# First expert pair of a routed SwiGLU layer: three column blocks side by side, with the gather between them

## The chip, the cores and the metric

The kernel runs on one core of one Trainium2 chip. The metric is device time in microseconds (us) of one execution, as the median over runs. A profiled execution also gives a span, from the first to the last instruction of the program.

## The reference

One post-norm encoder layer in float32 over 512 tokens of width 1024: LayerNorm, a mixer (short gated convolution and windowed attention), a residual and a second LayerNorm, then the part that the change touches, a mixture of 16 experts in which each expert picks its own 64 tokens:

```python
def expert_choice_moe(x, w_router, w_gate, w_up, w_down):
    B, S, _ = x.shape
    cap = CAPACITY_FACTOR * S // N_EXPERTS
    logits = jnp.einsum('bsd,de->bse', x, w_router).astype(jnp.float32)
    aff = jax.nn.softmax(logits, axis=-1)
    top_val, top_idx = lax.top_k(jnp.swapaxes(aff, 1, 2), cap)
    xe = x[b_idx, top_idx]
    h = jax.nn.silu(jnp.einsum('becd,edf->becf', xe, w_gate)) * jnp.einsum('becd,edf->becf', xe, w_up)
    ye = jnp.einsum('becf,efd->becd', h, w_down) * top_val[..., None].astype(x.dtype)
    return jnp.zeros_like(x).at[b_idx, top_idx].add(ye)
```

A residual and a last LayerNorm follow. The expert weights are 16 x 3 x 1024 x 2048 floats, 402.7 MB.

## The kernel before, in words

**Stages.** The mixer runs first and streams its weights through SBUF pools that are closed behind it. Then come routing (ranks, thresholds and places of the tokens, on VectorE) and the experts, in eight pairs `p`. Two experts of a pair sit side by side in 64 + 64 columns.

**A pair.** `gather(p)` builds a one-hot matrix `oh1` in the tile `px_p` (VectorE, L895) and returns a list of steps: eight row blocks of gathered tokens (`g`, TensorE L903, each then copied into `xe`) and a transposed one-hot (`oht`, L918). The hidden width of 2048 goes in four blocks of columns `cb`. In a block there are eight weight units of 1 MB (gate and up alternate, `i`; four quarters of the depth, `kq`), and each is used by 8 TensorE matmuls (`pg`, `pu`, L993; the order lists count two column halves as one row of 4). After a block come `silu` on ScalarE (L1003), the product on VectorE (L1004), and a step `turn` that transposes `h` (`ht`, L1016). Then 16 units of the down projection (`d`, L1042), and the scatter (`sc`, L1055). So a pair has 48 units.

**What sets the order on TensorE.** All its instructions are pinned to the order in which the program is written. Side steps wait in the list `pend`; the loop over units pops some between two units. In pair 0, block 0 pops two after each up unit, so that gathers come in twos; all later blocks pop one after each gate unit. When the block `cb == 1` of pair 0 ends, `pend` gets four steps of `spread` (`ln`, L929: TensorE writes the gain and bias of the second LayerNorm into PSUM, ScalarE copies each to the tile `ln1`, L930; the first two steps are the gain, the last two the bias) and then `affine` (L971 to L974), eight GpSimd instructions that multiply the four token tiles `xt` by the gain and add the bias, in place. Pair 0 has gathered its rows before that and applies gain and bias to them by itself; all later pairs gather from the finished `xt`.

**Between the pairs.** At the end of the four blocks `gather(1)` is called, and two of its steps (`g_1_0`, `g_1_2`) and the last `turn` run at once, ahead of the first `d`. Its tile `px_1` lies in the buffer W0, where `ln1` lies until `affine` is done, so VectorE's L895 for pair 1 waits for the last of GpSimd's instructions.

**Loads.** SyncE issues the weight loads in the order of the list, and each waits for its place. Units 0 to 71 (`SMALL`) are loads of 1 MB into places of 8 KB a partition: E, R0 to R19, W2, W0, so 23 units fit at first. After that W0 and W2 hold other tiles, and R0 and R1 become the accumulator, so that a unit from the 45th on goes into the place of the one 19 earlier. From unit 72 on four buffers G0 to G3 of 4 MB each take a group of four units with one load; they lie on R2 to R17, four places each. So the load of units 72 to 75 (into G2) waits until unit 56 has been used, the next until unit 60, and the load of units 80 to 83 (into G0) until unit 67.

Of the kernel before, what the change touches and what calls it, by code (L numbers as in the profile page):

```python
# [22 lines left out]
KT = D // P  # L23
# [8 lines left out]
NCB = FF // 512  # L32
# [7 lines left out]
def encoder_layer(ctx: ExitStack, tc: tile.TileContext, x, ln0r, ln0c, w_in, conv_w, sink, w_ao, w_co, w_out,  # L40
                  ln1c, w_router, w_moe, ln2c, out):
    nc = tc.nc
# [3 lines left out]
    extra = ctx.enter_context(tc.tile_pool(name="extra", bufs=1))  # L46
# [5 lines left out]
    pin = tc.keep_in_program_order  # L52

    def shaped(t, shape):
        names = "abcd"[:len(shape)]
        return t[:, :int(np.prod(shape))].rearrange(f"p ({' '.join(names)}) -> p {' '.join(names)}",
                                                    **dict(zip(names, shape)))

    def wkt(i, shape, name):
        return shaped(wk.tile([P, 2048], F32, tag=f"W{i % 3}", name=name), shape)  # L60
# [7 lines left out]
    def pst(name):  # L68
        return psp.tile([P, 512], F32, tag="ps", name=name)

    def mmt(name):
        return mmp.tile([P, 512], F32, tag="mm", name=name)
# [264 lines left out]
    src, nm, _ = loads[0]  # L337
# [244 lines left out]

    UNITS, SMALL = 48, 72
    units, groups = {}, {}

    def load_unit(n, pool, tag):
        t = pool.tile([P, 2048], F32, tag=tag, name=f"w_{n}")
        p, m = n // UNITS, n % UNITS  # L590
        pin(nc.sync.dma_start(t, w_moe[p, m // 4][:, m % 4]))
        return t

    def fetch(p, m):

        n = UNITS * p + m
        if n < SMALL:
            if n not in units:
                units[n] = load_unit(n, *places.pop(0))
            return units.pop(n)  # L600
        if not big:
            small.close()
            big.extend(ctx.enter_context(tc.tile_pool(name=f"big{i}", bufs=1, reuse_waits="tile")) for i in range(4))
            rest = ctx.enter_context(tc.tile_pool(name="late", bufs=1, reuse_waits="tile"))
            for name, shape, dt in (("c6", [P, KT, NT, 32], F32R), ("n6", [P, NT, 32], F32R), ("rows6", [P, D], F32R),
                                    ("left6", [P, P], F32R), ("diag", [P, P], F32)):
                late[name] = rest.tile(shape, dt, name=name)
        g, j = m // 4, m % 4
        if j == 0:
            i = (n // 4) % 4  # L610
            t = big[i].tile([P, 4, 2048], F32, tag=f"G{i}", name=f"w_{p}_{g}")
            src = w_moe[p, g]
            if p < NPAIR - 1 or g < 4:
                pin(nc.sync.dma_start(t, src))
            for i in range(4 if p == NPAIR - 1 and g >= 4 else 0):
                if (g, i) != (UNITS // 4 - 1, 3):
                    pin(nc.sync.dma_start(t[:, i], src[:, i]))
                else:
                    ends, begin = shaped(t[:, i], [2, 4, 256]), shaped(src[:, i], [2, 4, 256])
                    for f, n in ((0, 2), (2, 1), (3, 1)):  # L620
                        pin(nc.sync.dma_start(ends[:, :, f:f + n, :], begin[:, :, f:f + n, :]))
            groups[p, g] = t
        return groups[p, g][:, j]
# [255 lines left out]
    slots = [(accp, "R0"), (accp, "R1")]  # L879
    for i in range(2, 20):  # L880
        slots.append((small.enter_context(tc.tile_pool(name=f"r{i}", bufs=1, reuse_waits="tile")), f"R{i}"))
    places = slots[:7] + [(wk, "W2")] + slots[7:8] + [(wk, "W0")] + slots[8:]
    places += [(extra, "E")] + slots + [(extra, "E")] + slots[2:] + [(extra, "E")] + slots[2:10]
    big = []
    for n in range(1, 23):
        units[n] = load_unit(n, *places.pop(0))

    def gather(p):
# [74 lines left out]
    pend = []  # L963
# [16 lines left out]
    for p in range(NPAIR):  # L980
        last = p == NPAIR - 1
        xe, ohT, takes = nxt
        pend[:0] = takes
        for cb in range(NCB):
            pss = [mmt(f"p{nm}_{p}_{cb}") for nm in "gu"]
            for kq in range(4):
                for i in range(2):
                    wt = shaped(fetch(p, 8 * cb + 2 * kq + i), [2, 2, 512])
                    for k in range(2):
                        kk = 2 * kq + k  # L990
                        for a in range(2):
                            hs = slice(64 * a, 64 * a + 64)
                            pin(nc.tensor.matmul(pss[i][hs, :], xe[:, kk, hs], wt[:, a, k, :], start=(kk == 0), stop=(kk == KT - 1)))  # L993
                    for _ in range(2 * i if p == cb == 0 else 1 - i):
                        if pend:
                            pend.pop(0)()
            if last and cb == 1:
                ln2 = wkt(2, [1, D], "ln2")
                pend.extend(spread(ln2, 4, 2))
                ln2 = ln2[:, 0, :]  # L1000
                pend.extend(last_rows())
            hb = tmpt([512], f"h_{p}_{cb}")
            nc.scalar.activation(hb, pss[0], AF.Silu)  # L1003
            nc.vector.tensor_tensor(hb, hb, pss[1], OP.mult)  # L1004
            if p == 0 and cb == 1:
                ln1 = wkt(0, [2, D], "ln1")
                pend.extend(spread(ln1, 2))
                pend.append(affine)

            def turn(cb=cb, hb=hb, p=p):  # L1010
                if cb == 0:
                    hTs[p] = wkt(2 + 2 * p, [FF // P, P], f"hT_{p}")
                hT = hTs[p]
                ps = pst(f"ht_{p}_{cb}")
                for i in range(4):
                    pin(nc.tensor.transpose(ps[:, i * P:(i + 1) * P], hb[:, i * P:(i + 1) * P], ident))  # L1016
                nc.scalar.copy(hT[:, 4 * cb:4 * cb + 4, :].rearrange("p k c -> p (k c)"), ps)

            pend.append(turn)
            if last and cb == 2:  # L1020
                def begin(i):
                    def go():
                        ps = pst(f"end{i}")
                        pin(nc.tensor.matmul(ps, ident, acc[i][:, :, 768:1024], start=True, stop=False))
                        ends.extend(ps[:, 256 * t:256 * t + 256] for t in range(2))
                    return go
                pend.extend(begin(i) for i in range(2))
        if not last:
            nxt = gather(p + 1)
            for _ in range(2):  # L1030
                nxt[2].pop(0)()
            flush()
        nq, width = (4, 256) if last else (2, 512)
        for cq in range(nq):
            pd = mmt(f"d_{p}_{cq}")
            for fq in range(16 // nq):
                wt = shaped(fetch(p, 32 + 16 // nq * cq + fq), [2, nq, width])
                for ft in range(nq):
                    f = nq * fq + ft
                    for a in range(2):  # L1040
                        hs = slice(64 * a, 64 * a + 64)
                        pin(nc.tensor.matmul(pd[hs, :width], hTs[p][:, f, hs], wt[:, a, ft, :], start=(f == 0), stop=(f == 15)))  # L1042
                for _ in range(2):
                    if pend:
                        pend.pop(0)()
            ye = tmpt([width], f"ye_{p}_{cq}")
            nc.scalar.copy(ye, pd[:, :width])  # L1047
            if p == 0 and cq == 0:
                acc = [shaped(accp.tile([P, 2048], F32, tag=f"R{i}", name=f"acc{i}"), [2, D]) for i in range(2)]

            def scatter(t, p=p, cq=cq, ye=ye, ohT=ohT, width=width):
                def go():
                    cs = slice(cq * width, (cq + 1) * width)
                    ps = pst(f"sc_{p}_{cq}_{t}")
                    pin(nc.tensor.matmul(ps[:, :width], ohT[:, t * P:(t + 1) * P], ye, start=True, stop=True))  # L1055
                    a = acc[t // 2][:, t % 2, cs]
                    if p == 0:
                        nc.vector.scalar_tensor_tensor(a, xt[t][:, cs], ALPHA, ps[:, :width], op0=OP.mult, op1=OP.add)
                    else:
                        nc.vector.tensor_tensor(a, a, ps[:, :width], OP.add)  # L1060
                    if p == NPAIR - 1:
                        nc.vector.bn_stats(st2[:, t, cq, :], a)
                        nc.vector.tensor_tensor(a, a, ln2[:, cs], OP.mult)
                return go

            if last and cq == 0:
                pin(nc.scalar.preload_act_table(AF.Sqrt))
            if not (last and cq == 3):
                pend.extend(scatter(t) for t in range(NT))
# [96 lines left out]
```

## Time and profile before

| | us |
|---|---|
| median of 3 runs | 1443.61 (1443.17 to 1448.71) |
| the profiled execution, its own time | 1443.45 |
| its span | 1441.7 |
| TensorE busy in the span | 1365.8 (95%) |
| VectorE, ScalarE, GpSimd busy | 387.0, 290.5, 56.4 |

The profile has a page (busy time, 40 slices, the chain that ended last, the costliest groups) and a trace that answers by stretch, by engine and by tile. In a row of a stretch, "DMA share" is the mean busy share of the core's 16 DMA engines, and GB/s what they moved.

### The profile page before, as it was taken

What the parts mean: (1) busy time and instruction counts of PE and PEld (TensorE: products, weight loads), DVE (VectorE), ACT (ScalarE), POOL (GpSimd) and SP (SyncE); (2) the same over time, 40 slices, a digit from 0 to 9 for tenths busy, and PEclk for the clock granted to TensorE, in tenths of its full rate; (3) what the DMA queues carried; (4) which work ended last, traced back from release to release, by engine and by line L of the source; (5) the groups of instructions that cost most, each with busy time, mean ns of one, the idle gap of its engine ahead of it and who ended that gap; (6) DMA issues with size and microseconds to landing.
All of it is one profiled execution on the core that took longest, in us unless ns stands there. A gap on an engine that the chain in (4) does not pass through costs nothing.

```text
span 1441.7 us, 15527 instructions
## 1 busy us (share of the span) xinstructions
PE 1365.8 (95%) x6586; PEld 739.4 (51%) x6586; DVE 387.0 (27%) x854; ACT 290.5 (20%) x568; POOL 56.4 (4%) x44
## 2 busy tenths in 40 slices
PE   7999999999999999999999898889889889889997
PEld 6878787788888843433333332333323233233344
DVE  8566666633335340011010011011011001001114
ACT  5654454522324221100000000000000000000110
POOL 3000000230000002200000000000000000000000
PEclk9999999999999999999999999999999999999999
DMA  4221222322336879999999999999999999999995
GB/s 151 93 82 59 88 87 70 136 88 88 117 117 241 356 279 385 421 421 425 428 435 430 428 434 431 430 431 431 431 431 430 433 427 431 436 427 431 417 421 212
DMA packets 37093, 450.96 MB, mean 313 GB/s; under 512 B 4512, under 2 KB 7200, under 8 KB 10016
## 3 DMA queue, kind: packets, MB, share of 16 engines
q1 hardware_dynamic: 35728, 446.28, 74.8%
q10 hardware_dynamic: 1296, 3.69, 0.7%
q8 instruction: 52, 0.85, 0.2%
q14 instruction: 17, 0.14, 0.0%
HBM read 447.85 MB, written 2.10 MB: 312 GB/s over the span
## 4 chain that ended last, share of the span: by engine, by line
PE 69%; DMA 27%; DVE 3%; ACT 1%; issue 0%; DVEq 0%; SPq 0%
DMA w<-in_w_moe 26%; PE pu L993 10%; PE pg L993 10%; PE d L1042 8%; PE g L903 4%; PE p_x L183 3%; PE p_b L183 3%; PE p_c L183 3%; PE p_q L183 3%; PE p_co L183 3%; PE p_ao L183 3%; PE p_gc L183 3%; PE sc L1055 3%; PE p_ga L183 3%; PE o L524 1%; PE s L484 1%
## 5 line engine op out<-in xcount | busy, mean ns | idle before, releaser
L993 PE MATMUL pg<-w,px 128*64 128x512 f32 x1024 | 245.2, 600 | 33.3 <-DMA w<-in_w_moe 33.3
L1042 PE MATMUL d<-w,hT 128*64 128x512 f32 (+1 forms) x1152 | 232.1, 553 | 23.8 <-DMA w<-in_w_moe 23.7
L993 PE MATMUL pu<-w,px 128*64 128x512 f32 x1024 | 245.8, 601 | 0.0
L1042 PEld LDWEIGHTS d<-w,hT 128*64 128x64 f32 x1152 | 82.9, 137 | 164.1 <-issue 152.4
L993 PEld LDWEIGHTS pg<-w,px 128*64 128x64 f32 x1024 | 72.3, 137 | 183.8 <-issue 142.8
L993 PEld LDWEIGHTS pu<-w,px 128*64 128x64 f32 x1024 | 66.1, 136 | 130.1 <-issue 127.8
L1060 DVE TENSOR_TENSOR acc<-acc,sc 128x512 f32<-128x512 f32 (+1 forms) x60 | 38.1, 635 | 294.8 <-PE sc L1055 294.7
L1004 DVE TENSOR_TENSOR h<-h,pu 128x512 f32<-128x512 f32 x32 | 22.0, 688 | 317.3 <-PE pu L993 317.3
L1003 ACT ACTIVATE h<-pg 128x512 f32<-128x512 f32 x32 | 19.1, 598 | 311.9 <-PE pg L993 293.9
L903 PEld LDWEIGHTS g<-px,xn 128*128 128x128 f32 x512 | 59.0, 192 | 20.5 <-issue 19.5
L1055 PE MATMUL sc<-ye,px 128*128 128x512 f32 (+1 forms) x136 | 66.8, 597 | 0.0
L1047 ACT COPY ye<-d 128x512 f32<-128x512 f32 (+1 forms) x18 | 9.7, 539 | 275.0 <-PE d L1042 275.0
L903 PE MATMUL g<-px,xn 128*128 128x128 f32 x512 | 63.8, 280 | 0.2 <-DVE px L895 0.2
L1055 PEld LDWEIGHTS sc<-ye,px 128*128 128x128 f32 x136 | 22.2, 191 | 45.4 <-issue 44.3
L183 PE MATMUL p_x<-yh,ws_x 128*128 128x512 f32 x128 | 43.9, 398 | 0.0
L183 PE MATMUL p_b<-yh,ws_b 128*128 128x512 f32 x128 | 43.9, 398 | 0.0
L183 PE MATMUL p_c<-yh,ws_c 128*128 128x512 f32 x128 | 43.8, 398 | 0.0
L183 PE MATMUL p_q<-yh,ws_q 128*128 128x512 f32 x128 | 42.1, 395 | 0.0
L496 ACT ACTIVATE pr<-pr,neg 128x256 f32<-128x256 f32 (+1 forms) x64 | 35.2, 553 | 28.7 <-DVE neg L492 28.7
L183 PE MATMUL p_ga<-yh,ws_ga 128*128 128x512 f32 x128 | 40.6, 391 | 0.0
L183 PE MATMUL p_gc<-yh,ws_gc 128*128 128x512 f32 x128 | 40.1, 389 | 0.0
L183 PE MATMUL p_ao<-oh,ws_ao 128*128 128x512 f32 x128 | 40.1, 389 | 0.0
(282 smaller groups left out, 1616.6 us busy)
## 6 DMA issues: line engine op xcount, KB each, us to landing
w<-in_w_moe SPq DMA_DIRECT2D x70, 4096.0 KB, 29.4
w<-in_w_moe SPq DMA_DIRECT2D x103, 1024.0 KB, 13.2
raw_q<-in_w_in SPq DMA_DIRECT2D x4, 1024.0 KB, 4.7
raw_c<-in_w_in SPq DMA_DIRECT2D x4, 1024.0 KB, 4.8
raw_x<-in_w_in SPq DMA_DIRECT2D x4, 1024.0 KB, 4.7
raw_b<-in_w_in SPq DMA_DIRECT2D x4, 1024.0 KB, 4.8
raw_ga<-in_w_in SPq DMA_DIRECT2D x4, 1024.0 KB, 4.9
raw_gc<-in_w_in SPq DMA_DIRECT2D x4, 1024.0 KB, 4.9
```

The costliest lines, as they stand in the source:

```text
L183: put(nc.tensor.matmul(ps, ws[:, a, k, :], (opnd.lo if b else opnd.hi)(k), start=(k + a + b == 0), stop=ends))
L484: nc.tensor.matmul(ps, q, k[:, g, keys], start=(i == 0), stop=(i == 1))
L496: nc.scalar.activation(p, p, AF.Exp, bias=self.neg[:, i:i + 1], accum_out=self.su[:, i:i + 1])
L524: nc.tensor.matmul(pa[half * 64:half * 64 + 64, :256], vt[g][:, self.b0 + j, :], self.pT[:, j, :, half, :], start=(j == 0), stop=(j == sel ...
L903: pin(nc.tensor.matmul(ps[:, i * P:(i + 1) * P], xt[t][:, (k + i) * P:(k + i + 1) * P], oh1[:, t].rearrange("p a c -> p (a c)"), start=(t ...
L993: pin(nc.tensor.matmul(pss[i][hs, :], xe[:, kk, hs], wt[:, a, k, :], start=(kk == 0), stop=(kk == KT - 1)))
L1003: nc.scalar.activation(hb, pss[0], AF.Silu)
L1004: nc.vector.tensor_tensor(hb, hb, pss[1], OP.mult)
L1042: pin(nc.tensor.matmul(pd[hs, :width], hTs[p][:, f, hs], wt[:, a, ft, :], start=(f == 0), stop=(f == 15)))
L1047: nc.scalar.copy(ye, pd[:, :width])
L1055: pin(nc.tensor.matmul(ps[:, :width], ohT[:, t * P:(t + 1) * P], ye, start=True, stop=True))
L1060: nc.vector.tensor_tensor(a, a, ps[:, :width], OP.add)
```

## The change

In pair 0 the blocks 0, 1 and 2 are now worked on together: for each quarter of the depth, gate and up of block 0, then of block 1, then of block 2, with six accumulators in PSUM (the three up accumulators come from the other PSUM pool). Gather steps are popped one at a time, after the up unit of blocks 0 and 1. The three `silu`, product and `turn` steps follow after the last quarter, and with them the four `spread` steps and `affine`. Block 3 then pops two steps after each gate unit. The first 23 loads come in the new order of use, and units 72 to 79 are single loads too.

```diff
-    UNITS, SMALL = 48, 72
+    UNITS, SMALL = 48, 80
...
-    places += [(extra, "E")] + slots + [(extra, "E")] + slots[2:] + [(extra, "E")] + slots[2:10]
+    places += [(extra, "E")] + slots + [(extra, "E")] + slots[2:] + [(extra, "E")] + slots[2:18]
     big = []
-    for n in range(1, 23):
+    FIRST = 3
+    order = [8 * cb + 2 * kq + i for kq in range(4) for cb in range(FIRST) for i in range(2)]
+    for n in order[1:23]:
         units[n] = load_unit(n, *places.pop(0))
...
-        for cb in range(NCB):
-            pss = [mmt(f"p{nm}_{p}_{cb}") for nm in "gu"]
-            for kq in range(4):
-                for i in range(2):
...
-                    for _ in range(2 * i if p == cb == 0 else 1 - i):
-                        if pend:
-                            pend.pop(0)()
+        for cbs in ([0, 1, 2], [3]) if p == 0 else ([cb] for cb in range(NCB)):
+          several = len(cbs) > 1
+          acs = {cb: [mmt(f"pg_{p}_{cb}"), (pst if several else mmt)(f"pu_{p}_{cb}")] for cb in cbs}
+          for kq, cb in [(kq, cb) for kq in range(4) for cb in cbs]:
+            for i in range(2):
+                wt = shaped(fetch(p, 8 * cb + 2 * kq + i), [2, 2, 512])
...
+                for _ in range((i if cb != cbs[-1] else 0) if several else (1 - i) * (2 if p == 0 else 1)):
+                    if pend:
+                        pend.pop(0)()
+          for cb in cbs:
+            pss = acs[cb]
```

TensorE at the start of pair 0, before (names: `g_0_k` is row block k of the gather, `pg_0_cb` and `pu_0_cb` are gate and up of block cb, `w_n` is weight unit n):

```order
L903 MATMUL g_0_1_4294<-px_0_4283,xn1_2528 128x128 x2
L993 MATMUL pg_0_0_4300<-w_0_3390,px_0_4283 64x512 x4
L993 MATMUL pu_0_0_4301<-w_1_4237,px_0_4283 64x512 x4
L903 MATMUL g_0_2_4310<-px_0_4283,xn0_2527 128x128 x2
L903 MATMUL g_0_2_4310<-px_0_4283,xn1_2528 128x128 x2
L903 MATMUL g_0_3_4316<-px_0_4283,xn0_2527 128x128 x2
L903 MATMUL g_0_3_4316<-px_0_4283,xn1_2528 128x128 x2
L993 MATMUL pg_0_0_4300<-w_2_4239,px_0_4283 64x512 x4
L993 MATMUL pu_0_0_4301<-w_3_4241,px_0_4283 64x512 x4
```

The same place in the changed kernel:

```order
L905 MATMUL g_0_1_4294<-px_0_4283,xn1_2528 128x128 x2
L997 MATMUL pg_0_0_4300<-w_0_3390,px_0_4283 64x512 x4
L997 MATMUL pu_0_0_4301<-w_1_4237,px_0_4283 64x512 x4
L905 MATMUL g_0_2_4314<-px_0_4283,xn0_2527 128x128 x2
L905 MATMUL g_0_2_4314<-px_0_4283,xn1_2528 128x128 x2
L997 MATMUL pg_0_1_4302<-w_8_4239,px_0_4283 64x512 x4
L997 MATMUL pu_0_1_4303<-w_9_4241,px_0_4283 64x512 x4
L905 MATMUL g_0_3_4328<-px_0_4283,xn0_2527 128x128 x2
L905 MATMUL g_0_3_4328<-px_0_4283,xn1_2528 128x128 x2
L997 MATMUL pg_0_2_4304<-w_16_4243,px_0_4283 64x512 x4
L997 MATMUL pu_0_2_4305<-w_17_4245,px_0_4283 64x512 x4
L997 MATMUL pg_0_0_4300<-w_2_4247,px_0_4283 64x512 x4
```

Between two units of block 0 there now stand one gather step and the units of two other blocks, where two gather steps stood.

TensorE in block 2 of pair 0, before; the rows `ln` are the `spread` steps, the third and fourth of which come two and four units later:

```order
L993 MATMUL pg_0_2_4425<-w_16_4267,px_0_4283 64x512 x4
L929 MATMUL ln_4431<-ident_98,cols_89 128x128 x4
L993 MATMUL pu_0_2_4426<-w_17_4269,px_0_4283 64x512 x4
L993 MATMUL pg_0_2_4425<-w_18_4271,px_0_4283 64x512 x4
L929 MATMUL ln_4445<-ident_98,cols_89 128x128 x4
L993 MATMUL pu_0_2_4426<-w_19_4273,px_0_4283 64x512 x4
```

TensorE in block 3 of pair 0 in the changed kernel, up to the gather of pair 1:

```order
L997 MATMUL pg_0_3_4457<-w_24_4459,px_0_4283 64x512 x4
L1022 MATMUL ht_0_0_4466<-ident_98,h_0_0_4447 128x128 x4
L931 MATMUL ln_4472<-ident_98,cols_89 128x128 x4
L997 MATMUL pu_0_3_4458<-w_25_4478,px_0_4283 64x512 x4
L997 MATMUL pg_0_3_4457<-w_26_4484,px_0_4283 64x512 x4
L931 MATMUL ln_4490<-ident_98,cols_89 128x128 x4
L931 MATMUL ln_4496<-ident_98,cols_89 128x128 x4
L997 MATMUL pu_0_3_4458<-w_27_4502,px_0_4283 64x512 x4
...
L997 MATMUL pu_0_3_4458<-w_31_4552,px_0_4283 64x512 x4
L905 MATMUL g_1_0_4566<-px_1_4561,xn0_2527 128x128 x2
```

Between the second `spread` step and the gather of pair 1 stood thirteen units (19 to 31); now there are five (27 to 31).

## Rows read from the trace of the kernel before

**Rows 1.** The page, its first part: busy time by engine.
```profile
PE 1365.8 (95%) x6586; PEld 739.4 (51%) x6586; DVE 387.0 (27%) x854; ACT 290.5 (20%) x568; POOL 56.4 (4%) x44
```

**Rows 2.** Stretches: busy time by engine, granted clock, DMA share, GB/s.
```profile
core 0: us, PE busy (x) PEld busy (x) DVE busy (x) ACT busy (x) POOL busy (x), PEclk, DMA share, GB/s
523.50:548.00 24.50, 24.50 (x140) 12.49 (x140) 3.34 (x9) 3.01 (x6) 0.00 (x0) 1.00 0.79 275
548.00:573.00 25.00, 25.00 (x122) 8.87 (x122) 0.69 (x1) 2.94 (x5) 4.87 (x3) 1.00 0.99 393
...
760.00:1416.00 656.00, 599.27 (x2832) 225.44 (x2828) 59.73 (x109) 48.44 (x90) 0.00 (x0) 0.99 1.00 429
...
600.00:640.00 40.00, 40.00 (x190) 15.35 (x188) 4.34 (x9) 1.92 (x4) 0.00 (x0) 1.00 1.01 421
...
720.00:760.00 40.00, 40.00 (x187) 14.89 (x188) 5.72 (x11) 2.52 (x5) 0.00 (x0) 1.00 1.00 430
```

**Rows 3.** Waits of PE in the whole span, then from 523 to 760 us.
```profile
PE pg L993 <- DMA w<-in_w_moe: 33.3, 21, 2.7
PE d L1042 <- DMA w<-in_w_moe: 23.7, 16, 2.6
...
PE g L903 <- DVE px L895: 0.2, 1, 0.2
```

**Rows 4.** The chain that ended last, in pair 0: start, us, what.
```profile
523.45 2.02 PE g L903 x16
525.48 1.87 PE pg L993 x8
527.34 1.72 PE pu L993 x8
529.06 1.98 PE g L903 x16
...
566.85 0.58 PE ln L929 x4
...
592.84 3.77 PE g L903 x32
```

**Rows 5.** Timeline of POOL, 540 to 640 us: start, us, what, idle before.
```profile
568.13 9.31 POOL L973 TENSOR_TENSOR xn<-xn,ln 128x1024 f32<-128x1024 f32 x4 [116.39 <-ACT ln L930]
577.39 9.32 POOL L974 TENSOR_TENSOR xn<-xn,ln 128x1024 f32<-128x1024 f32 x4
```

**Rows 6.** Timeline of DVE, 523 to 632 us: the one-hots of pairs 0 and 1.
```profile
523.01 0.90 DVE L895 TENSOR_TENSOR px<-iota,place 128x128 f32<-128x128 f32 x4
...
586.74 0.90 DVE L895 TENSOR_TENSOR px<-iota,place 128x128 f32<-128x128 f32 x4 [8.31 <-POOL xn L974]
```

**Rows 7.** Tile w on SyncE's queue, three single loads: issue, time to landing.
```profile
L591 SPq DMA_DIRECT2D w<-in_w_moe x1: 328/328/328, 527.4 to 527.4; - x1
...
DMA to landing us min/median/max: 5.0/5.0/5.0
...
L591 SPq DMA_DIRECT2D w<-in_w_moe x1: 328/328/328, 599.0 to 599.0; - x1
...
DMA to landing us min/median/max: 9.3/9.3/9.3
...
L614 SPq DMA_DIRECT2D w<-in_w_moe x1: 327/327/327, 674.5 to 674.5; - x1
...
DMA to landing us min/median/max: 14.1/14.1/14.1
```

**Rows 8.** Timeline of PE after waits of 1.79 and 2.72 us.
```profile
892.66 1.94 PE L993 MATMUL pg<-w,px 128*64 128x512 f32 x8 [1.79 <-DMA w<-in_w_moe]
...
1255.23 3.43 PE L993 MATMUL pg<-w,px 128*64 128x512 f32 x8 [2.72 <-DMA w<-in_w_moe]
```

**Rows 9.** A stretch behind another such wait: columns as in rows 2.
```profile
824.80:828.20 3.40, 3.40 (x8) 0.81 (x8) 0.00 (x0) 0.00 (x0) 0.00 (x0) 0.50 0.98 424
```

More of the change, by code (lines that the diff above doesn't have):

```diff
@@ L983, in encoder_layer @@
         pend[:0] = takes
-        for cb in range(NCB):
-            pss = [mmt(f"p{nm}_{p}_{cb}") for nm in "gu"]
-            for kq in range(4):
-                for i in range(2):
[L988 to L993, printed above, removed]
-                    for _ in range(2 * i if p == cb == 0 else 1 - i):
-                        if pend:
-                            pend.pop(0)()
+        for cbs in ([0, 1, 2], [3]) if p == 0 else ([cb] for cb in range(NCB)):
[4 more added lines that the diff above has]
+                wt = shaped(fetch(p, 8 * cb + 2 * kq + i), [2, 2, 512])
+                for k in range(2):
+                    kk = 2 * kq + k
+                    for a in range(2):
+                        hs = slice(64 * a, 64 * a + 64)
+                        pin(nc.tensor.matmul(acs[cb][i][hs, :], xe[:, kk, hs], wt[:, a, k, :], start=(kk == 0), stop=(kk == KT - 1)))
+                for _ in range((i if cb != cbs[-1] else 0) if several else (1 - i) * (2 if p == 0 else 1)):
[3 more added lines that the diff above has]
+            pss = acs[cb]
             if last and cb == 1:
```

## The prediction

> **What bounds the kernel now.** The page's first part is read first: TensorE is busy 95% of the span [rows 1], which would make it the bound; but the matmuls are pipelined, so a stage is judged by its waits. The list of TensorE's waits says that in the whole span it waits for almost nothing but expert weights, 33.3 us ahead of gate units and 23.7 us ahead of down units, and that between 523 and 760 us it waits for nothing that counts [rows 3]. The stretches say why [rows 2]: from 760 us to the end of the weights the DMA engines are busy all the time at 429 GB/s. So the last part of the kernel ends when the last weight has landed, and a load that lands later by some time at 690 us makes the end later by the same time, since no idle DMA time is left in which to catch up. From 523 to 760 us it is the other way round: TensorE never stops, the loads wait for places that TensorE sets free, and the DMA engines have idle time only up to about 560 us: 275 GB/s from 523.5 to 548 and 393 GB/s to 573, against 421 with single loads in a full queue (600 to 640) and 430 with loads of 4 MB (720 to 760) [rows 2]. The question is what the change does to the time at which places come free, from the first unit to unit 67, whose place is the last that the first load of 4 MB into G0 needs.
>
> **Part 1, the order of units and gathers.** Sixteen gather matmuls take 1.98 us as a piece of the chain, thirty-two 3.77 [rows 4]: 1.79 for sixteen more, hence 0.19 for starting a piece, and a single step (eight matmuls) costs 0.90 + 0.19 = 1.09. A unit takes 1.87 behind such a piece and 1.72 otherwise [rows 4]. Before, two units cost 1.98 + 1.87 + 1.72 = 5.57, or 2.79 each. Now six units stand with two single steps: 2 x 1.09 + 2 x 1.87 + 4 x 1.72 = 12.8, or 2.13 each. A load of 1 MB needs 1.049 MB / 421 GB/s = 2.49 us, so that the DMA engines, starved before, are no longer starved. Before, the eight units of block 0 are used at 523.45 + 4 x 5.57 = 545.7; by then some ten are used now. Two places more, at 2.49 each, are a lead of about **5 us** for the loads. TensorE's own sum hardly moves: the number of side pieces is 12 in both orders (four double gathers, one `oht`, three `ht`, four `ln` before; seven gather pieces, one `oht`, four pieces of `ht` and `ln` now), so the gather of pair 1 would be reached at 592.8 [rows 4], give or take 0.3.
>
> **Part 2, what becomes of the lead.** The load that leaves at 599.0 (unit 51, into the place of unit 32, the first down unit) lands 9.3 us later; a load into an empty queue takes 5.0 [rows 7]. With the loads ahead of it 5 us earlier, at most 9.3 - 5.0 = 4.3 us of the lead pass this place. The load of units 80 to 83 leaves at 674.5 and lands 14.1 us later. Into an empty queue it would need 4.19 MB / 430 GB/s = 9.75 us, and the 5.0 - 2.49 = 2.5 us that the single load takes beyond its own transfer: 12.3. So at most 14.1 - 12.3 = **1.8 us** can be gained behind unit 67, whatever is gained before. This is the cap of the change's good side.
>
> **Part 3, eight single loads for two groups.** Eight take 8 x 2.49 = 19.9 us, two groups 2 x 9.75 = 19.5 [rows 2]. The 0.4 us lies ahead of the load of units 80 to 83, which waits for unit 67 anyway; it is hidden, and if that cover went, it would cost 0.4. The rows at 600 us show a queue full of single loads at 421 GB/s, which leaves no room for a fixed cost in each. The Trainium skill would price it otherwise (DMA: Bandwidth & Descriptors, section Anatomy of one DMA, a fit made on the GpSimd path): about 2.0 us fixed for each DMA beside its bytes; six more DMAs would be 12 us by that, if nothing hid it. The single load of 5.0 us agrees with such a fixed part; the 421 GB/s do not.
>
> **Part 4, `spread` and `affine`.** This is the step that I think decides. The second `spread` step is what GpSimd waits for. It ended at 566.85 + 0.58 = 567.43 [rows 4], GpSimd began at 568.13, 0.70 later (the copy on ScalarE lies between), and its eight instructions ran without a gap to 577.39 + 9.32 = 586.71 [rows 5]: 18.6 us. VectorE's one-hot of pair 1 began at 586.74, released by GpSimd [rows 6], and the gather began at 592.84 [rows 4], so there were some 5.7 us to spare.
>
> Now only this stands between the second `spread` step and that gather: the third step in the same piece (0.45, eight matmuls less one start and four matmuls), units 27 to 31 (three behind a side piece, two not: 3 x 1.87 + 2 x 1.72 = 9.05), the fourth step (0.58) and a piece of two `ht` (1.03): 11.1 us. TensorE reaches the gather at 592.8, so the second step ends at 581.7. GpSimd begins 0.70 later, at 582.4, and ends at 601.0. VectorE starts its one-hot at once; from there to the first gather matmul 0.44 us pass, as in pair 0 (523.01 to 523.45) [rows 6, 4]. **The gather of pair 1 begins at 601.5 instead of 592.84, 8.7 us late**, and TensorE stands still in front of it. All its later work is pinned behind: `ht` of block 3, the down units, and with them the places from unit 32 on. On VectorE the product of block 3 is queued behind the one-hot; only that late `ht` needs it, which comes 3.8 us after the gather's start.
>
> Such a wait costs more than itself. Behind a wait of 2.72 us a unit took 3.43 us instead of 1.94 behind one of 1.79 [rows 8], and in such a place the granted clock was 0.50, which is 1.2 GHz, until it rose again [rows 9]. One drop costs 1.5 us by these rows. The wait here is three times as long as the longest of rows 3; it may cost 0 (if the clock rises before it matters) to 3.0 (two drops). I take 2.0, a little over one.
>
> **The sum**, against the profiled execution's 1443.45. TensorE is late by 8.7 + 2.0 = 10.7 us from the gather on, and has no wait until 760 in which to make that up. The load of unit 51 leaves at 599.0 + 10.7 = 609.7, into a queue that has run dry, and lands at 614.7; the 28 single loads behind it need 28 x 2.49 = 69.7 and land by 684.4 or a little later. The load of units 80 to 83 leaves at 674.5 + 10.7 = 685.2, so that its queue is just empty: it lands 12.3 to 14.1 us later, and I take 12.6, near the empty queue. That is 697.8, against 674.5 + 14.1 = 688.6 before: **+9.2 us**, which all later loads and the end inherit. 1443.45 + 9.2 = 1452.65, so 1452.6; the median of the three runs shown, 1443.61, is 0.2 above the profiled execution, which changes nothing. Bounds of the same case: no clock loss and 12.3 give 8.7 - 1.8 = +6.9 (1450.4), two drops and 14.1 give 11.7 (1455.2).
>
> **The rivals.**
> A, the wait does not come, and the kernel is not slower. It decides by the time at which GpSimd begins: with 18.6 us of work and 0.5 behind it, a start before 592.8 - 19.1 = 573.7 leaves TensorE alone. Then only the cap of part 2 counts: 1443.45 - 1.8 = 1441.6. Against it: the order on TensorE puts five units between, and five units are 9 us. For it: only that my working of 582.4 is not measured. 0.10.
> B, the wait comes but the lead of part 1 is kept beside it, because places bind less than rows 7 make me think: 10.7 - 5 = 5.7, 1449.1. Against it: during the wait no place comes free, so any lead runs out. 0.12.
> C, single loads cost a fixed part each that the queue does not hide. By rows 7 that part is 2.5 us, six of them 15: the loads end at 699.4 instead of 684.4 and the group behind lands 9.75 later, at 709.2, +20.6: 1464. Rows 2 speak against it, the fit of the Trainium skill's page in part 3 for it. 0.02.
> D, the wait costs the clock more than two drops, or the thin queue behind it loses time at every load: +13 to +16, 1456.5 to 1459.5. 0.06.
>
> **How the numbers follow.** The forecast has 0.70. A measurement of this kernel can tell 0.5%, 7.2 us, from no change: slower means over 1450.8. Of the forecast 0.67 lies above this and 0.03 below; C and D add 0.08: slower 0.75. B and most of A (0.09) and the 0.03 make no difference that could be told: 0.24. Faster by over 0.5% would need more than the cap: 0.01. The range from 1448 to 1456.5 holds the forecast, most of B and the near edge of D, some 0.8.
>
> **What would show it.** Right: GpSimd's L975 begins at about 582 and ends at about 601; the list of waits has a new wait of `g` for `px` of 8 to 9 us; granted clock 0.50 right behind it; the load of unit 51 leaves at about 610; the first load of 4 MB leaves at about 685; DMA rate above 400 GB/s from 530 to 590, then a hole at 602 to 611. Wrong: GpSimd begins before 574, or the gather does not wait for `px`; or the loads behind unit 67 land less than 6 us later than before.

## The result, and the profile after

| | before | after |
|---|---|---|
| median | 1444.59 us (6 runs, 1442.91 to 1448.71) | 1453.7 us (6 runs, 1453.12 to 1458.12) |
| profiled execution, span | 1441.7 us | 1451.7 us |
| ratio after / before | | 1.0068, 95% interval 1.0055 to 1.0082 |

The changed kernel is 0.68% slower: 9.8 us by the ratio (7.9 to 11.8), 9.1 by the medians, 10.0 by the spans. The forecast was +9.2 us, slower by over 0.5%.

The stages ahead of the experts, which no kernel here touches, end some microseconds later in some executions: the gather of pair 0 began between 523.2 and 525.1 us in nine of the twelve profiles, and between 527.7 and 528.4 in three. Such an execution is longer by as much as a whole: the one of the version with 72 small loads and no wait (below) starts 5.1 us later than that of the same kernel with 80, and its span is 1446.3 us instead of 1441.4. Where a kernel's inner times are compared with another's, a large offset of this kind is taken off and named; the changed kernel's own is 0.4 us against the kernel before.

The view to read first is the list of TensorE's waits, in the whole span of the changed kernel (engine, tile and line, what it waited for, us in total, times, longest):

```profile
PE pg L997 <- DMA w<-in_w_moe: 29.9, 19, 2.7
PE d L1048 <- DMA w<-in_w_moe: 23.3, 15, 4.0
PE g L905 <- DVE px L897: 8.7, 2, 8.5
```

In total the two waits for weights are no longer than in [rows 3] (29.9 and 23.3 us against 33.3 and 23.7), so the added time does not lie in them. New is one wait of 8.5 us of the gather for the one-hot `px`. Its place on the timelines of GpSimd, VectorE and TensorE (start, us, what, idle before and its releaser):

```profile
583.06 9.31 POOL L975 TENSOR_TENSOR xn<-xn,ln 128x1024 f32<-128x1024 f32 x4 [131.06 <-ACT ln L932]
592.32 9.24 POOL L976 TENSOR_TENSOR xn<-xn,ln 128x1024 f32<-128x1024 f32 x4
```

```profile
601.59 0.90 DVE L897 TENSOR_TENSOR px<-iota,place 128x128 f32<-128x128 f32 x4 [25.34 <-POOL xn L976]
```

```profile
591.50 1.94 PE L997 MATMUL pu<-w,px 128*64 128x512 f32 x8
601.93 5.65 PE L905 MATMUL g<-px,xn 128*128 128x128 f32 x32 [8.50 <-DVE px L897]
607.42 0.60 PE L1022 MATMUL ht<-ident,h 128*128 128x128 f32 x4
607.95 4.51 PE L1048 MATMUL d<-w,hT 128*64 128x512 f32 x20
```

GpSimd's eight instructions take as long as before [rows 5] and start 14.9 us later; VectorE's one-hot follows their end within 0.03 us, as in [rows 6]; and TensorE, done with its last unit at 593.4, stands still until 601.93. The gather behind that takes 5.65 us instead of 3.77 [rows 4]. The stretches (columns as in [rows 2]) show the clock and the DMA engines there:

```profile
523.50:548.00 24.50, 24.34 (x131) 11.14 (x130) 1.69 (x6) 1.37 (x3) 0.00 (x0) 1.00 0.79 306
548.00:573.00 25.00, 25.00 (x123) 9.45 (x124) 2.79 (x5) 2.24 (x4) 0.00 (x0) 1.00 0.99 394
595.51:605.75 10.24, 3.82 (x18) 3.82 (x19) 1.50 (x5) 0.00 (x0) 6.04 (x3) 0.50 0.61 254
604.10:609.90 5.80, 5.80 (x38) 4.45 (x39) 0.00 (x0) 1.33 (x3) 0.00 (x0) 0.86 0.00 0
...
760.00:1416.00 656.00, 604.27 (x2808) 223.91 (x2808) 58.16 (x101) 48.70 (x90) 0.00 (x0) 0.98 1.00 430
```

The granted clock is 0.50 (1.2 GHz) from 595.5, during the wait, to 605.8, so most of the gather runs at half speed. The DMA engines stand still from 604.1 to 609.9, because no place has come free since the wait began, and from 760 us on they run as fast as before, with nothing idle in which to catch up. What the two loads of the prediction did is in SyncE's queue (issue, then time to landing); the third is the load of units 88 to 91:

```profile
L591 SPq DMA_DIRECT2D w<-in_w_moe x1: 327/327/327, 609.9 to 609.9; - x1
...
DMA to landing us min/median/max: 5.0/5.0/5.0
...
L614 SPq DMA_DIRECT2D w<-in_w_moe x1: 328/328/328, 685.4 to 685.4; - x1
...
DMA to landing us min/median/max: 12.1/12.1/12.1
...
L614 SPq DMA_DIRECT2D w<-in_w_moe x1: 328/328/328, 699.9 to 699.9; - x1
...
DMA to landing us min/median/max: 18.4/18.4/18.4
```

Unit 51's load leaves 10.9 us later than in [rows 7] and finds an empty queue; the load of units 80 to 83 leaves 10.9 us later and lands at 697.5, 8.9 us later than before. Two loads later the distance is 10.3 us (718.3 against 708.0), and the end keeps that, with 10.0 us between the spans. Why 8.9 became 10.3 is taken up below, where the lead of the new order is followed.

### The profile page after: what moved, and what is told of

Read it like the earlier page. It is cut to its first block, busy times and chain, and to the rows that moved or that the text cites. A ratio compares the mean times of both kernels' runs of the same rounds, so it can differ in the third digit from the quotient of the medians.

```text
span 1451.7 us, 15537 instructions
## 1 busy us (share of the span) xinstructions
PE 1370.9 (94%) x6586; PEld 742.2 (51%) x6586; DVE 386.9 (27%) x854; ACT 290.2 (20%) x568; POOL 56.3 (4%) x44
## 4 chain that ended last, share of the span: by engine, by line
PE 65%; DMA 24%; issue 7%; DVE 2%; POOL 1%; ACT 1%; SPq 0%; DVEq 0%; POOLq 0%
DMA w<-in_w_moe 23%; PE pu L997 9%; PE pg L997 9%; PE d L1048 9%; PE sc L1061 3%; PE p_x L183 3%; PE p_b L183 3%; PE p_c L183 3%; PE g L905 3%; PE p_q L183 3%; PE p_co L183 3%; PE p_ao L183 3%; PE p_gc L183 3%; PE p_ga L183 3%; PE o L524 1%
## 5 line engine op out<-in xcount | busy, mean ns | idle before, releaser
L997 PE MATMUL pg<-w,px 128*64 128x512 f32 x1024 | 245.6, 600 | 30.0 <-DMA w<-in_w_moe 29.9
L1048 PE MATMUL d<-w,hT 128*64 128x512 f32 (+1 forms) x1152 | 234.7, 558 | 23.3 <-DMA w<-in_w_moe 23.3
## 6 DMA issues: line engine op xcount, KB each, us to landing
w<-in_w_moe SPq DMA_DIRECT2D x111, 1024.0 KB, 12.9
```

Source lines behind the costliest of these rows:

```text
L997: pin(nc.tensor.matmul(acs[cb][i][hs, :], xe[:, kk, hs], wt[:, a, k, :], start=(kk == 0), stop=(kk == KT - 1)))
```

## The experiments

The theory: the late second `spread` step, and it alone, makes the kernel slower, by a wait in front of the gather of pair 1 and the clock behind it, and the loads pass both on to the end. The rivals: the eight single loads or the new order cost time of their own; the wait is made up before 760 us and the time went elsewhere.

**Take the wait away.** `spread` and `affine` move ahead, and from the second quarter of the depth on a side step is popped after block 2's up unit too; the order of units, the loads and the places stay.

```diff
...
+        if p == 0:
+            def lay():
+                ln1s.append(wkt(0, [2, D], "ln1"))
+                pend[:0] = spread(ln1s[0], 2) + [affine]
+                pend.pop(0)()
+            pend.append(lay)
...
-                for _ in range((i if cb != cbs[-1] else 0) if several else (1 - i) * (2 if p == 0 else 1)):
+                for _ in range((i if kq or cb != cbs[-1] else 0) if several else (1 - i) * (2 if p == 0 else 1)):
...
-            if p == 0 and cb == 1:
-                ln1 = wkt(0, [2, D], "ln1")
-                pend.extend(spread(ln1, 2))
-                pend.append(affine)
```

> The changed kernel, but with the three-block order, the 80 small loads and the places as they are, and only the two spread steps and the affine moved: they are issued right behind the gather steps of pair 0, so that GpSimd starts at about 569 us instead of 583. Theory (the late GpSimd work makes TensorE wait in front of the gather of pair 1, and that wait alone makes the kernel slower): no wait of g for px, gather of pair 1 begins at about 593, granted clock 1.00 there, the load of units 80 to 83 leaves at about 675 and lands at about 687; total 1442.5 to 1444, that is 10 us under the changed kernel and 0 to 2 us under the one before. Rival (the eight single loads or the new order of units cost the time, and the wait would have been made up anyway): over 1449, with the same wait-free gather.

Measured: ratio to the kernel before 0.9997 (0.9986 to 1.0007), median 1444.05. Timelines of GpSimd and TensorE:

```profile
569.93 9.31 POOL L976 TENSOR_TENSOR xn<-xn,ln 128x1024 f32<-128x1024 f32 x4 [118.40 <-ACT ln L932]
```

```profile
593.28 3.84 PE L905 MATMUL g<-px,xn 128*128 128x128 f32 x32
```

GpSimd starts 13.1 us earlier than in the changed kernel (0.7 of it is the start of the execution), the gather does not wait, and the whole loss is gone. The rival that the rest of the change costs the time is out: by the interval it costs at most 1 us and gains at most 2. That no gain is seen either is taken up below.

**Make the wait in the kernel before.** Only the place of `spread` and `affine` is changed; block 3 pops two steps after each gate unit, as in the changed kernel.

```diff
-                    for _ in range(2 * i if p == cb == 0 else 1 - i):
+                    for _ in range(2 * i if p == cb == 0 else (1 - i) * (2 if p == 0 and cb == 3 else 1)):
...
-            if p == 0 and cb == 1:
+            if p == 0 and cb == 2:
                 ln1 = wkt(0, [2, D], "ln1")
```

> The kernel before with nothing changed but the place of the two spread steps and the affine: they are issued one block of columns later, two steps to a gate unit, so that the second spread step ends at about 579 us. Theory: GpSimd runs from about 579.5 to 598, the gather of pair 1 waits 5 to 6 us for px and begins at about 598.5, the clock drops once (1.5 to 2 us more), and the first load of 4 MB into G0 leaves some 7 us later: total 1450 to 1452, 6 to 7.5 us over the kernel before, without any of the change's other parts. Rival (the wait is made up before 760 us, and the change's time went elsewhere): within 2 us of the kernel before.

Measured: 1.0051 (1.0031 to 1.0072), that is +7.4 us. TensorE's timeline and waits from 523 to 760 us:

```profile
602.49 6.24 PE L903 MATMUL g<-px,xn 128*128 128x128 f32 x32 [5.58 <-DVE px L895]
```

```profile
PE g L903 <- DVE px L895: 5.7, 2, 5.6
```

The wait is 5.6 us and the gather takes 6.24 instead of 3.77, 2.5 us more: 8.1 in all. Less the offset of 4.7 us (this execution's first gather began at 528.1), TensorE comes to the wait 0.5 us earlier than the kernel before comes to its gather, and the load of units 80 to 83 leaves at 681.9, 7.4 later than in [rows 7]. The kernel before is made slower by the same mechanism, without any other part of the change.

**Make the wait longer.** In the changed kernel the three `turn`s of blocks 0 to 2 go ahead of `spread`.

```diff
-                pend.extend(spread(ln1, 2))
-                pend.append(affine)
+                late1 = spread(ln1, 2) + [affine]
...
             pend.append(turn)
+            if p == 0 and cb == 2:
+                pend.extend(late1)
```

> The changed kernel, but with the three transposes of h of blocks 0 to 2 queued ahead of the spread steps instead of behind, so that GpSimd starts about 4.6 us later still. Theory (time follows the wait one to one): the wait of g for px grows from 8.5 to about 13 us, the load of units 80 to 83 leaves at about 690, total about 1458.3, 4.6 us over the changed kernel. Rival (something else sets the end, and the wait is partly hidden): within 1.5 us of the changed kernel.

Measured: 1.0104 (1.0087 to 1.0120), 5.2 us more than the changed kernel's 1.0068. The gather's row, one of its matmuls missing from the records:

```profile
607.73 5.44 PE L905 MATMUL g<-px,xn 128*128 128x128 f32 x31 [13.08 <-DVE px L897]
```

The wait has grown by 4.6 us. With waits of 5.6, 8.5 and 13.1 us the kernels are 7.4, 9.8 and 15.0 us slower than the one before: the wait comes through in full, with one to two us on top.

**Part the wait from its clock.** Extra matmuls, which write a tile that nobody reads, stand in front of the gather of pair 1 and keep TensorE busy while GpSimd works.

```diff
         if not last:
+            if p == 0:
+                fill = pst("fill")
+                for _ in range(68):
+                    pin(nc.tensor.matmul(fill[:, :P], ident, ident, start=True, stop=True))
             nxt = gather(p + 1)
```

> The changed kernel with 68 extra matmuls of 128 columns in front of the gather of pair 1, which write a tile that nobody reads; TensorE is busy for most of the time in which it otherwise stands still for 8.5 us. It tells what of the 10 us lies in the wait itself and what in the clock behind it. Theory (the clock's part is about 1.9 us, the 32 gather matmuls taking 5.65 us instead of 3.77): granted clock stays at 1.00, the gather takes 3.8 us, total about 1451.8, 1.9 us under the changed kernel. Rival 1 (the slower gather is hidden): 1453.7, no change. Rival 2 (the extra matmuls run at half the clock and end after GpSimd): over 1455.

Measured: 1.0100 (1.0083 to 1.0117), 4.6 us over the changed kernel. TensorE's timeline, then the stretch of the extra matmuls:

```profile
593.06 15.45 PE L1038 MATMUL fill<-ident 128*128 128x128 f32 x136
608.35 3.74 PE L905 MATMUL g<-px,xn 128*128 128x128 f32 x32
```

```profile
593.06:608.35 15.29, 15.29 (x138) 15.29 (x137) 1.50 (x5) 0.00 (x0) 8.24 (x4) 1.00 0.56 234
```

The second rival's time, but not for its reason: the extra matmuls ran at full clock (1.00), and were simply too many. A matmul of the program is two of the rows' instructions, and 68 took 15.45 us where 8.5 were to be filled. The gather began 6.4 us later than in the changed kernel and took 1.9 less, 4.5 us against the 4.6 measured. With 37 instead of 68 the fill ends when the one-hot is there:

> The changed kernel with 37 extra matmuls of 128 columns in front of the gather of pair 1, which write a tile that nobody reads; 68 of them took 15.45 us at full clock and ended 6.4 us after GpSimd would have let the gather begin, so 37 take 8.4 us and end with it. Theory: the gather begins at about 602 as in the changed kernel, granted clock 1.00, takes 3.75 us instead of 5.65, and the end comes 1.9 us earlier than in the changed kernel: 1451.8. Rival (the slower gather behind the wait is hidden): 1453.7.

Measured: 1.0047 (1.0029 to 1.0065), median 1452.06. TensorE's timeline, then the stretch in which the changed kernel had 0.50:

```profile
593.43 8.53 PE L1038 MATMUL fill<-ident 128*128 128x128 f32 x74
602.03 3.88 PE L905 MATMUL g<-px,xn 128*128 128x128 f32 x32
```

```profile
595.50:605.75 10.25, 10.18 (x91) 9.99 (x91) 1.50 (x5) 0.37 (x1) 6.15 (x3) 1.00 0.61 252
```

The gather begins at the same time as in the changed kernel (602.03 and 601.93) and ends 1.7 us earlier; the load of units 80 to 83 leaves at 683.8 instead of 685.4, and the median is 1.6 us lower. By the ratios it is 3.0 us, with intervals that overlap; the trace is the sharper witness here. Of the lateness, 8.5 us are the wait and some 1.8 its clock.

**The eight single loads alone.** The changed kernel, and the one without the wait, each with 72 small loads.

```diff
-    UNITS, SMALL = 48, 80
+    UNITS, SMALL = 48, 72
...
-    places += [(extra, "E")] + slots + [(extra, "E")] + slots[2:] + [(extra, "E")] + slots[2:18]
+    places += [(extra, "E")] + slots + [(extra, "E")] + slots[2:] + [(extra, "E")] + slots[2:10]
```

> The changed kernel with 72 small loads instead of 80, all else as it is. Theory: the wait of 8.5 us stays, the load of units 80 to 83 leaves at 685.4 and lands at 697.5 as in the changed kernel: 1453.7, within 1 us of it. Rival (the single loads cause part of the slow-down): 1440 to 1451.

> The changed kernel with the spread steps and the affine issued early, and 72 small loads as before instead of 80. Theory (the load of units 80 to 83 waits for unit 67 either way, so the eight single loads cost and give nothing): units 80 to 83 land at 687 to 687.5, total within 1 us of the run with 80. Rival (a fixed cost per single load): 2 to 15 us under it.

Measured: 1.0071 (1.0049 to 1.0094) against the changed kernel's 1.0068, and 1.0004 (0.9992 to 1.0017) against 0.9997. Both executions have the late start (3.8 and 5.1 us). Less that, the load of units 80 to 83 leaves at 686.1 and at 675.0, where the kernels with 80 have 685.4 and 675.0. The single loads neither cost nor give anything that can be told; in the first of the two the 0.7 us is the gather, which took 6.30 us instead of 5.65 behind the same wait:

```profile
605.76 6.30 PE L905 MATMUL g<-px,xn 128*128 128x128 f32 x32 [8.50 <-DVE px L897]
```

**Where the lead of the new order goes.** Without the wait the loads are ahead of the kernel before: unit 50's lands at 603.1 (593.4 + 9.7) instead of 605.8 (592.9 + 12.9), 2.6 us. Unit 50 in the kernel before, then without the wait:

```profile
L591 SPq DMA_DIRECT2D w<-in_w_moe x1: 327/327/327, 592.9 to 592.9; - x1
...
DMA to landing us min/median/max: 12.9/12.9/12.9
```

```profile
L591 SPq DMA_DIRECT2D w<-in_w_moe x1: 328/328/328, 593.4 to 593.4; - x1
...
DMA to landing us min/median/max: 9.7/9.7/9.7
```

Nothing of that is seen at the end. The rows around unit 80 show why, first the kernel before (the load ahead of units 80 to 83, and two behind them), then the version without the wait (the load ahead, units 80 to 83, two behind):

```profile
L614 SPq DMA_DIRECT2D w<-in_w_moe x1: 328/328/328, 659.8 to 659.8; - x1
...
DMA to landing us min/median/max: 19.1/19.1/19.1
...
L614 SPq DMA_DIRECT2D w<-in_w_moe x1: 328/328/328, 688.9 to 688.9; - x1
...
DMA to landing us min/median/max: 19.1/19.1/19.1
```

```profile
L591 SPq DMA_DIRECT2D w<-in_w_moe x1: 327/327/327, 660.3 to 660.3; - x1
...
DMA to landing us min/median/max: 15.5/15.5/15.5
...
L614 SPq DMA_DIRECT2D w<-in_w_moe x1: 328/328/328, 675.0 to 675.0; - x1
...
DMA to landing us min/median/max: 12.2/12.2/12.2
...
L614 SPq DMA_DIRECT2D w<-in_w_moe x1: 328/328/328, 689.5 to 689.5; - x1
...
DMA to landing us min/median/max: 18.3/18.3/18.3
```

Before, the load ahead lands at 678.9 and units 80 to 83 at 688.6 [rows 7], 9.7 later, the pace of a full queue. Without the wait the load ahead lands at 675.8, but units 80 to 83 at 687.2, 11.4 later: their load needs four places at once, unit 67's the last, and leaves at 675.0, only 0.8 us before the load ahead has landed. The DMA engines run short of work there. From 674.5 to 678 the version without the wait has this row, and the version below with four single loads in that place the second (columns as in [rows 2]):

```profile
674.50:678.00 3.50, 3.50 (x20) 1.15 (x16) 0.00 (x0) 0.00 (x0) 0.00 (x0) 1.00 0.78 257
674.50:678.00 3.50, 3.50 (x18) 1.15 (x16) 0.00 (x0) 0.00 (x0) 0.00 (x0) 1.00 1.00 410
```

That hole is 1.7 us. Two loads later 707.8 stands against 708.0: nothing of the lead is left. In the kernel before, the landing at 678.9 had come 1.5 us behind the pace (11.3 us behind the one ahead of it, at 667.6, instead of 9.7), and without the wait such a landing, 1.1 us late, comes only now, at 707.8. So of the 3.0 us between 675.8 and 678.9 only 1.5 are lead, and the hole takes all of it. The changed kernel meets its late landing at the same load: its units 88 to 91 land 11.1 us behind the ones ahead, which is why its distance grew from 8.9 to 10.3 us. If the hole is what takes the lead, four more single loads, each waiting for one place, should keep it:

```diff
-    UNITS, SMALL = 48, 80
+    UNITS, SMALL = 48, 84
...
-    places += [(extra, "E")] + slots + [(extra, "E")] + slots[2:] + [(extra, "E")] + slots[2:18]
+    places += [(extra, "E")] + slots + [(extra, "E")] + slots[2:] + [(extra, "E")] + slots[2:18] + slots[2:6]
```

> The changed kernel with the spread steps and the affine issued early (as in the run before that took the wait away), and units 80 to 83 as four single loads more (84 in all) instead of one load of 4 MB. In the run without the wait the queue still ran empty there: unit 79 landed at 675.8, the load of units 80 to 83 left at 675.0 when unit 67 was used, and landed at 687.2, 11.4 us behind, where a load of 4 MB in a full queue takes 9.7. Theory (the lead of the new order is lost in this hole of about 1.7 us, because one load of 4 MB waits for four places at once): four single loads leave as each place comes free, the queue stays full, unit 83 has landed at about 685.8, 1.4 us earlier, and all later loads keep it: total about 1442.6, 2 us under the kernel before. Rival (each single load costs a fixed part that the queue does not hide): 1444 to 1452.

Measured: 0.9983 (0.9970 to 0.9996); 2.5 us under the kernel before, between 0.6 and 4.3. The load of unit 83:

```profile
L591 SPq DMA_DIRECT2D w<-in_w_moe x1: 328/328/328, 675.0 to 675.0; - x1
...
DMA to landing us min/median/max: 11.0/11.0/11.0
```

It lands at 686.0, 1.2 us ahead of the same unit in the version with 80, 2.5 us behind unit 82's and with no hole. It keeps that: units 164 to 167 land at 891.3, where the version with 80 and the kernel before both have 892.6. So the hole accounts for 1.2 to 1.3 of the 2.5 us; the rest lies within the interval and is not explained. Two controls go with it: the kernel before with 84 small loads, and 88 in the version without the wait.

> The kernel before with 84 small loads instead of 72, in its own order of units. It tells whether the 2 us that the early spread steps with 84 small loads gained come from the new order of units (a lead of 2.6 us at 603 us) or from the small loads alone. Theory: in the kernel before the queue never ran empty at units 80 to 83, so there is no hole to close: 12 single loads take 29.9 us where three of 4 MB take 29.2, units 80 to 83 land within 1 us of 688.6, total within 1 us of the kernel before. Rival (the small loads alone give the gain): 2 us faster than the kernel before.

> The changed kernel with early spread steps and 88 small loads. Theory: with 84 the hole is closed, and units 84 to 87 as one load of 4 MB left 4.2 us before the load ahead of it landed, into a queue that was not empty, so four more single loads find no hole: within 0.7 us of the version with 84. Rival (the hole only moved one load further): 1 us or more faster than with 84.

Measured: 0.9997 (0.9984 to 1.0010) for the first; unit 83 lands at 688.7 against 688.6, though single landings differ by more than a microsecond between executions. In the kernel before there is no hole, and 84 small loads give nothing that can be told. The second: 0.9991 (0.9980 to 1.0002), 1.2 us above the version with 84, more than the 0.7 expected but within the intervals; units 84 to 87 land one by one and units 88 to 91 then 9.7 us behind, so no second hole is seen. That 84 beats the kernel before is shown by its own interval alone, and by little: the intervals of 84 overlap those of both controls and of the version with 80, so that the gain needs the new order and the closed hole is what the landings say, not yet the times.

## Why the prediction was right

- **Part 4, the step that decides, held number by number.** GpSimd began at 583.06 (forecast 582.4) and ended at 601.56 (601.0), the gather began at 601.93 (601.5), the wait was 8.5 us (8.7). Taking the wait away, making it in the kernel before, and lengthening it moved the time as it says.
- **The price of the clock was 1.9 us where I took 2.0.** It is the gather's 5.65 less 3.77 (1.8 against the 3.84 that the timeline without the wait has), and keeping TensorE busy gave 1.7 of it back. My two rows stood for units behind shorter waits, and I guessed the number of drops, so that the 2.0 came this close is in part luck. What counts is how long TensorE works at half speed: here from 601.93 to 605.75, 3.8 us, and half of that is lost.
- **The sum.** TensorE was late by 8.5 + 1.9, and by 10.9 at unit 51 and at units 80 to 83, of which 0.4 is the later start of this execution. The load of units 80 to 83 took 12.1 us to land where I took 12.6, just under my empty-queue bound of 12.3; that is why it landed at 697.5 instead of 697.8. But the step from there to the end, that all later loads inherit the +9.2, was about 1 us short: my 14.1 us for the kernel before held a late landing of 1.5 us, which the changed kernel met two loads later. Without it the load gained about 0.5 us over the kernel before and not 1.5, and the end came 10.0 later by the spans, 9.8 by the ratio. The range covers that; the sum did not have it.
- **Part 1 was nearly twice too large.** I forecast a lead of 5 us; it was 2.6, and in the changed kernel itself 1.7 (unit 50 at 604.0), or 2.2 less its later start. The stretch to 548 us gained as it should (306 GB/s, 317 without the wait, against 275 in [rows 2]); the next did not: 394 and 390 GB/s against 393, and over the 530 to 590 of my sign it is 403, just above the 400. My count of units was nearly right (the tenth was done at 547.0, 546.5 less the later start); the step that failed is taking each for a full transfer at the rate of a full queue. This error cost the forecast nothing, since the wait uses up any lead, as rival B's paragraph had said.
- **Part 2, the cap, was right at its own load, but it is not what a version without the wait gets.** The 14.1 to 12.3 that I read as 1.8 us came out as 14.1 to 12.2, and units 80 to 83 landed 1.4 us earlier. Rival A's 1441.6 is then still too low: 1.1 of the 1.4 was gone two loads later, so its real time is that of the kernel before. The row of 14.1 us held a late landing that every version meets once somewhere near.
- **Part 3 held:** with 72 or 84 small loads the times agree. About 2.0 us fixed for each DMA (the Trainium skill, DMA: Bandwidth & Descriptors, section Anatomy of one DMA, a fit on the GpSimd path) does not show in a full queue of SyncE here: twelve single loads in place of three large ones in the kernel before gave 0.9997. Only where the queue ran empty was there a loss, the hole of 1.7 us.
- Rival D, more than two drops or losses in the thin queue, did not come; it would have been over 1456.5.

## What to carry to other kernels

When steps are interleaved anew, follow the longest chain on the slow engines from its last input: here a reorder that touched only TensorE and loads moved the input of 18.6 us of GpSimd work by 15 us, of which 5.7 were spare. Where the stage behind is bound by transfers, as here from 760 us on, the lateness counts at the next place that loads wait for, and nothing behind it makes it up. One large load that needs several places at once can lose a lead that small ones, each with one place, would keep; look for an interval between two landings that is longer than the pace of a full queue.

## What was not expected of the hardware

- The granted clock was already 0.50 when the gather started: it fell at 595.5, during the wait, and rose at 605.8. What it costs doesn't grow with the wait. In the kernel before with the late `spread` the stretch at half speed is this (columns as in [rows 2]):

```profile
600.73:607.56 6.83, 5.07 (x24) 5.08 (x25) 1.50 (x5) 0.37 (x1) 1.38 (x1) 0.50 1.02 423
```

  Here 5.1 us of the gather lie in it, and it took 2.5 us longer than 3.77; behind the longer wait of 8.5 us 3.8 us lay in it, and it took 1.9 longer; behind 13.1 us again 3.6 (the clock was 0.50 until 611.3) and some 1.8. In the changed kernel with 72 small loads the wait is 8.5 us too, but 5.1 us of the gather lie at half speed, and it took 2.5 longer.
- The extra matmuls held the clock at 1.00 although they read and wrote nothing of use; for a wait that can't be removed this gives back 1.7 us. They have to end on time: every microsecond beyond the wait is paid in full.
- Three times between 670 and 1290 us, 225 to 255 us apart, in the kernel before and in most others, a load of 4 MB landed 1.0 to 1.7 us behind the pace of 9.7. The place differs between executions and shifts comparisons of single landings by as much. In the profiled execution of the version with 84 no load is late by so much at once; it falls back 1.3 us bit by bit against the kernel before, from units 104 to 107 until units 164 to 167. The cause was not tried.
